# A hybrid trunk layer on one core: six more merge gates as seven-product pairs, their block differences formed on POOL and kept in DRAM

## The chip, the cores and the metric

The kernel runs on one core of a Trainium2 chip. The metric is the device time of one execution in microseconds (us), as the median of several runs. Engines are named as in the profile: PE (TensorE), DVE (VectorE), ACT (ScalarE), POOL (GpSimd) and SP, the queue that issues most DMAs.

## What is computed

One layer of width 1024 over 1024 positions. A combined projection feeds three causal mixers (stick-breaking attention "sb", gated DeltaNet "gdn", gated linear attention "gla") and three merge gates; the gated mixer outputs are projected, weighted by the merge gates, summed and projected again.

```python
h = rms_norm(x, norm_g) * (1 + scale) + shift
(sq, sk, sv, sz, dq, dk_, dv_, dz, db, da,
 lq, lk, lv, lz, lr, mg) = jnp.split(h @ w_in, offsets, axis=-1)   # mg: 3 * 1024 columns
y_sb, y_gdn, y_gla = ...          # the mixers, each times its silu gate; 512, 512, 1024 wide
g_sb, g_gdn, g_gla = jnp.split(jax.nn.sigmoid(mg + merge_b), 3, axis=-1)
merged = g_sb * (y_sb @ proj_sb) + g_gdn * (y_gdn @ proj_gdn) + g_gla * (y_gla @ proj_gla)
return x + gate * (merged @ w_out)
```

## The kernel before

Activations lie transposed: a tile has 128 channels as partitions and 1024 positions as columns, HS being its two halves of 512. Every fp32 operand of a large product is split into a rounded part `hi` (a cast on ACT, L151) and the rest `lo` (a subtraction on DVE, L152), and a product is three matmuls, hi·hi, hi·lo and lo·hi. `h_hi` and `h_lo` are the eight split tiles of h. Weights come as raw tiles of 256 KB (8 buffers) and are split into `w` tiles.

Work comes in *dense groups*: projection columns (`D.…`), merge gates (`gate(gi, d)`: 128 columns of one of the three gates, two halves of 24 matmuls, evacuated on ACT in L1182, sigmoid in L1187, kept in DRAM as `g_dram`), and the groups of the end. The mixers' small chained steps (`G.…` gdn, `L.…` gla, `S.m0` to `S.m3` sb) run at the same time. `emit` walks a clock of its own through the program and puts pieces of dense groups as filler between the mixers' steps; only PE's order is fixed by it, the other engines' by the order of the code and a scheduler. `dense` loads one group ahead. `FILL` says how many of the 24 gates are put at ten places of that stream; the ones that are left belong to `final_groups`, which run only when `S.m3` is done, so with no mixer beside them: the left gates, with `gla_operands` in between; four `gla_pair`; eight `proj_group` of proj_gdn, eight of proj_sb, and four `out_pair`.

A *pair* (`strassen`) computes two row blocks of 128 output channels at once with seven block products instead of eight: the four weight blocks are combined on DVE (`part`: s1 to s4), the right side is given as seven *units* (b11, t1, t2, b22, t3, b21, t4) a block p of four, a unit being hi and lo of 128x512. A pair has 7 × 12 = 84 matmuls. `combine` forms the units of one block with four subtractions and seven splits. In `gla_operands` it reads the four quarters from `y_dram`, where the mixers left their outputs. In `proj_group` of proj_sb with d of 4 and more it makes the units of `out_pair` from the merged tiles. `load_y` fetches and splits the four tiles that proj_gdn or proj_sb multiplies, in halves by way of two `mid` tiles. In `proj_group` each half is multiplied by its gate (L1366) and added to the merged tile (L1367), both on DVE.

Where the prediction follows steps of a mixer: in gla, L907 to L920 are DVE's elementwise work of the level steps, L1006 and L1008 the state's update in the scan, L292 is a power (reciprocal root) on POOL and L805 its multiplication on DVE; in sb, L1123/L1124 are activations on ACT, L1125 a scan over the keys on DVE, L1127 a product, L122 transposes on PE, L1148 their copies to SBUF on DVE, then the products with v (`mx`).

Of the kernel before, what the change touches and what calls it, by code (L numbers as in the profile page):

```python
# [52 lines left out]
def kernel(ctx: ExitStack, tc: tile.TileContext, xT: bass.AP, c: bass.AP,  # L53
# [1153 lines left out]
    def combine(b11, b12, b21, b22, unit, t1, t2):  # L1207

        out = {}

        def put(name, src):
            u = out[name] = unit(name)
            split(u[:, 0:HALF], u[:, HALF:2 * HALF], src)

        put("b11", b11)
        nc.vector.tensor_sub(out=t1, in0=b12, in1=b11)
        put("t1", t1)
        nc.vector.tensor_sub(out=t2, in0=b22, in1=t1)
        put("t2", t2)
        put("b22", b22)  # L1220
        nc.vector.tensor_sub(out=b12, in0=b22, in1=b12)
        put("t3", b12)
        put("b21", b21)
        nc.vector.tensor_sub(out=b21, in0=b21, in1=t2)
        put("t4", b21)
        return out

    def strassen(src, n1, n2, rhs, prepare, read):
# [75 lines left out]
    def gla_operands(p):  # L1304
        def run(_):
            raws = []
            for k in (p, p + 4):
                for sl, tag in zip(HS, ("v2", "v3")):
                    t = mid(tag)
                    nc.sync.dma_start(out=t, in_=y_dram[8 + k][:, sl])  # L1310
                    raws.append(t)
            gla_c[p] = combine(*raws, lambda name: unit_tile(GLA_TAGS[name][p]),
                               mid("v4"), mid("v4"))
            return
            yield
        return (lambda: None), run
# [4 lines left out]

# [198 lines left out]
```

## Time and profile before

| | |
|---|---|
| runs | 1523.69, 1524.74, 1530.83 us; median 1524.74 |
| profiled execution | 1526.96 us, span 1525.2 |
| busy PE / DVE / ACT / POOL | 1452.1 / 932.1 / 698.8 / 170.5 us |
| granted TensorE clock, mean | 0.982 of full speed |
| mixers alone with dense filler | to about 1184 us of the span |
| gates left, gla pairs, proj_gdn, proj_sb, out pairs | to 1249, 1339, 1392, 1443 and 1525 us |

Busy times are sums over the whole span; what one stage is limited by is read from its own stretch, by the waits that end last there.

### The profile page before, as it was taken

Reading aid. Unit: us, or ns where it says so; the run is one execution under the profiler, and the core shown is the slowest. Engines: PE = TensorE matmul, PEld = TensorE weight load, DVE = VectorE, ACT = ScalarE, POOL = GpSimd, SP = SyncE. Lnnn points to the kernel's source line nnn. Section 1 sums busy time; section 2 is a strip of 40 time slices with the busy share of each in tenths; the row PEclk is TensorE's granted clock in tenths of the full one; section 3 lists DMA queues with packets and bytes.
Section 4 is the critical chain, followed back from the end, with each engine's and each line's share of the span. In section 5 each row is a group of like instructions: output and inputs, shape, how many; then the busy total and the mean of one; then the engine's idle time right before and its main releaser. Section 6 shows DMA issues by size and latency. Waiting matters only on the chain.

```text
span 1525.2 us, 26640 instructions
## 1 busy us (share of the span) xinstructions
PE 1452.1 (95%) x10468; PEld 1211.1 (79%) x10468; DVE 932.1 (61%) x1930; ACT 698.8 (46%) x1483; POOL 170.5 (11%) x307
## 2 busy tenths in 40 slices
PE   4898999999999999999999999999999989989898
PEld 1687787777778887979788999999988867868687
DVE  6988737566643756666666525563655347577973
ACT  5165835453643746566476524342433344332321
POOL 4221222222330000000000100000000000000000
PEclk8899999999999999999999999999999998999999
DMA  6743322231322111111212221111123334474351
GB/s 223 218 125 112 99 80 74 57 81 47 90 83 60 39 47 56 46 55 38 73 43 60 66 56 36 49 50 45 40 63 101 114 115 117 132 230 125 111 162 66
DMA packets 169383, 132.77 MB, mean 87 GB/s; under 512 B 24197, under 2 KB 140037, under 8 KB 169258
## 3 DMA queue, kind: packets, MB, share of 16 engines
q1 hardware_dynamic: 169114, 130.76, 29.6%
q8 instruction: 82, 1.34, 0.4%
q14 instruction: 43, 0.35, 0.1%
q10 hardware_dynamic: 144, 0.31, 0.1%
HBM read 102.94 MB, written 28.10 MB: 86 GB/s over the span
## 4 chain that ended last, share of the span: by engine, by line
PE 76%; DVE 11%; DMA 5%; ACT 4%; POOL 2%; issue 2%; SPq 0%; DVEq 0%; POOLq 0%; ACTq 0%
PE acc L95 62%; PE lv L95 6%; PE mx L95 5%; PE tr L122 2%; DMA u<-in_adaT 1%; DVE u L307 1%; DVE w L152 1%; DVE w L583 1%; DVE u L394 1%; DVE w L581 1%; DMA v<-y_dram 1%; DMA v<-gam_d 1%; DMA w<-xd 1%; POOL c L292 1%; POOL u L464 1%
## 5 line engine op out<-in xcount | busy, mean ns | idle before, releaser
L95 PE MATMUL acc<-h_hi,w 128*128 128x512 f32 x1856 | 656.5, 408 | 11.0 <-ACT h_hi L364 7.0
L95 PEld LDWEIGHTS acc<-h_hi,w 128*128 128x128 f32 x1856 | 351.7, 189 | 82.9 <-issue 8.0
L95 PE MATMUL acc<-h_lo,w 128*128 128x512 f32 x928 | 365.8, 394 | 9.4 <-DVE h_lo L366 7.8
L151 ACT CAST w<-raw 128x512 fp32r<-128x512 f32 x231 | 140.9, 619 | 234.2 <-PE acc L95 203.4
L95 PE MATMUL acc<-w,h_hi 128*128 128x256 f32 x1280 | 238.8, 287 | 0.0
L152 DVE TENSOR_TENSOR w<-raw,w 128x512 fp32r<-128x512 f32 x231 | 159.7, 699 | 128.4 <-ACT w L151 123.2
L95 PEld LDWEIGHTS acc<-h_lo,w 128*128 128x128 f32 x928 | 176.6, 190 | 38.8 <-DVE h_lo L366 9.0
L95 PEld LDWEIGHTS acc<-w,h_hi 128*128 128x128 f32 x1280 | 198.7, 191 | 1.5 <-issue 0.7
L95 PE MATMUL acc<-u,w 128*128 128x512 f32 x696 | 179.0, 406 | 18.3 <-ACT u L151 12.7
L95 PE MATMUL acc<-w,h_lo 128*128 128x256 f32 x640 | 180.7, 282 | 0.0
L95 PEld LDWEIGHTS acc<-u,w 128*128 128x128 f32 x696 | 134.1, 194 | 54.3 <-ACT u L151 18.1
L95 PEld LDWEIGHTS acc<-w,h_lo 128*128 128x128 f32 x640 | 122.1, 191 | 0.0
L292 POOL TENSOR_TENSOR c<-c,mhalf 128x4 f32<-128x4 f32 (+1 forms) x56 | 54.9, 980 | 597.7 <-DVE c L290 573.3
L95 PE MATMUL acc<-unit,w 128*128 128x512 f32 x360 | 92.2, 394 | 0.0
L95 PEld LDWEIGHTS acc<-unit,w 128*128 128x128 f32 x360 | 67.9, 189 | 15.6 <-ACT v L1329 0.3
L1182 ACT ACTIVATE v<-acc,col 128x512 f32<-128x512 f32 x48 | 32.9, 685 | 81.1 <-PE acc L95 80.6
L1125 DVE TENSOR_TENSOR_SCAN u<-u,zero_c 128x128 f32<-128x128 f32 (+7 forms) x32 | 43.4, 1357 | 41.1 <-ACT u L1123 41.1
L95 PEld LDWEIGHTS mx<-r,u 128*128 128x128 f32 x288 | 44.1, 190 | 18.4 <-DVE r L762 4.9
L95 PE MATMUL mx<-r,u 128*128 128x128 f32 x288 | 48.5, 281 | 6.8 <-DVE r L762 2.4
L95 PE MATMUL lv<-u,u 128*32 128x32 f32 (+5 forms) x528 | 48.7, 250 | 2.2 <-DVE u L664 2.2
L95 PEld LDWEIGHTS lv<-u,u 128*32 128x32 f32 (+2 forms) x528 | 40.1, 145 | 11.1 <-issue 6.6
L286 ACT COPY u<-acc 128x512 f32<-128x512 f32 x50 | 29.0, 581 | 42.0 <-PE acc L95 41.4
(270 smaller groups left out, 2009.3 us busy)
## 6 DMA issues: line engine op xcount, KB each, us to landing
raw<-in_w_in SPq DMA_DIRECT2D x160, 256.0 KB, 3.1
u<-in_adaT SPq DMA_DIRECT2D x24, 512.0 KB, 4.0
g_dram<-v SPq DMA_DIRECT2D x48, 256.0 KB, 2.2
v<-g_dram SPq DMA_DIRECT2D x48, 256.0 KB, 2.9
v<-y_dram SPq DMA_DIRECT2D x32, 256.0 KB, 3.5
u<-in_xT SPq DMA_DIRECT2D x8, 512.0 KB, 8.0
v<-gam_d SPq DMA_DIRECT2D x16, 256.0 KB, 3.2
y_dram<-v SPq DMA_DIRECT2D x16, 256.0 KB, 2.0
```

What stands on the lines that cost most here:

```text
L95: return nc.tensor.matmul(out, lhsT=lhsT, rhs=rhs, **kw)
L122: nc.tensor.transpose(out=out, in_=in_, identity=ident[:k, :k])
L151: nc.scalar.copy(out=hi, in_=raw)
L152: nc.vector.tensor_sub(out=lo, in0=raw, in1=hi.bitcast(F32))
L286: nc.scalar.copy(out=dst[:, sl], in_=ps)
L292: nc.gpsimd.tensor_tensor(out=out, in0=out, in1=mhalf[:, 0:n], op=ALU.pow)
L307: nc.vector.tensor_tensor_reduce(out=junk, in0=aw, in1=c_row, scale=1.0, scalar=0.0, op0=ALU.mult, op1=ALU.add, accum_out=mod[:, j:j + 1])
L394: nc.vector.scalar_tensor_tensor(out=t, in0=r[:, tap:tap + T], scalar=C("conv", j + tap), in1=t, op0=ALU.mult, op1=ALU.add)
L464: nc.gpsimd.tensor_scalar(out=gt[0][DA, sl], in0=raw[DA, :], scalar1=C("dt_bias")[DA, :], scalar2=None, op0=ALU.add)
L581: nc.vector.tensor_tensor(out=t3, in0=L3[:, w:16, j:w].broadcast_to([32, n, w]), in1=Xl3[:, j:w, 0:w].broadcast_to([32, n, w]), op=ALU.mult)
L1125: nc.vector.tensor_tensor_scan(om[:, 0:n][:, ::-1], om[:, 0:n][:, ::-1], zero_c.broadcast_to([P, n]), 1.0, ALU.mult, ALU.add)
L1182: nc.scalar.activation(out=g, in_=ps, func=AF.Identity, bias=C("merge_b", gi * 8 + d))
```

## The change

Four of the eighteen gates that were filler leave the mixers: two behind the last gla columns (FILL[6]), one behind D.S0, one behind D.S2. Of the ten gates now left for `final_groups` four stay plain, two ahead of and two behind three `gate_pair`, each of which computes two gates with the seven products. Their units need differences of quarters of h: `T.h0` to `T.h3` form them on POOL during the mixers (four additions, since h is kept split, and four subtractions a block) and write them to DRAM; `T.y0` to `T.y3` do the same for the gla outputs (four loads, four subtractions). `h_operands` (put ahead of the first plain gate) and `gla_operands` (in two waves, 19 units ahead of the third plain gate and 9 ahead of gla pair 0) then load each unit's raw quarter straight into the place of its lo part and split it there. `load_y` does so with whole tiles. In proj_sb the merged add of d below 6 goes from DVE to POOL, and t4 of the out units is formed in t2's tile.

```diff
-FILL = (5, 1, 4, 0, 0, 0, 2, 1, 1, 4)
+FILL = (5, 1, 4, 0, 0, 0, 0, 0, 0, 4)
+PLAIN = (2, 2)
...
+    def load_unit(tag, src):
+        hi, lo = new_unit(tag)
+        raw = lo.bitcast(F32)
+        nc.sync.dma_start(out=raw, in_=src)
+        nc.scalar.copy(out=hi, in_=raw)
+        nc.vector.tensor_sub(out=lo, in0=raw, in1=hi.bitcast(F32))
+        return hi, lo
...
+    def differences(n, p, get):
+        def flat():
+            return raw_tile().rearrange("p k n -> p (k n)")
+        def sub(out, a, b, t):
+            nc.gpsimd.tensor_sub(out=out, in0=a, in1=b)
+            nc.sync.dma_start(out=t_dram[n, p][t], in_=out)
+        b12, b11 = get(flat(), 0, 1), get(flat(), 0, 0)
+        sub(b11, b12, b11, "t1")
+        b22 = get(flat(), 1, 1)
+        sub(b12, b22, b12, "t3")
+        sub(b22, b22, b11, "t2")
+        b21 = get(flat(), 1, 0)
+        sub(b21, b21, b22, "t4")
...
+    def h_differences(p):
+        def get(out, i, j):
+            k, sl = p + 4 * i, HS[j]
+            nc.gpsimd.tensor_add(out=out, in0=h_hi[k][:, sl].bitcast(F32),
+                                 in1=h_lo[k][:, sl].bitcast(F32))
+            return out
+    def y_differences(p):
+        def get(out, i, j):
+            nc.sync.dma_start(out=out, in_=y_dram[8 + p + 4 * i][:, HS[j]])
+            return out
...
+    def h_operands():
+        for p in range(4):
+            h_c[p] = {name: (h_hi[k][:, sl], h_lo[k][:, sl])
+                      for name, k, sl in (("b11", p, HS[0]), ("b21", p + 4, HS[0]),
+                                          ("b22", p + 4, HS[1]))}
+        for t in ("t1", "t2", "t3", "t4"):
+            for p in range(4):
+                h_c[p][t] = load_unit(H_TAGS[t][p], t_dram["h", p][t])
...
+    def gate_pair(e1, e2):
+        ...
+        return strassen(*cols_, h_c, dict, read)
...
         for k, tag in enumerate(Y_TAGS[yi]):
             a, b = unit_tile(tag), unit_tile(tag)
-            for sl, v in zip(HS, ("v2", "v3")):
-                yr = mid(v)
-                nc.sync.dma_start(out=yr, in_=y_dram[yi + k][:, sl])
-                split(a[:, sl], b[:, sl], yr)
+            raw = b.bitcast(F32)
+            nc.sync.dma_start(out=raw, in_=y_dram[yi + k])
+            nc.scalar.copy(out=a, in_=raw)
+            nc.vector.tensor_sub(out=b, in0=raw, in1=a.bitcast(F32))
...
                 nc.vector.tensor_mul(out=t, in0=g[hf], in1=ps)
-                nc.vector.tensor_add(out=merged[d][:, sl], in0=merged[d][:, sl], in1=t)
+                add = nc.gpsimd if gi == 0 and d < 6 else nc.vector
+                add.tensor_add(out=merged[d][:, sl], in0=merged[d][:, sl], in1=t)
...
-        late = [gate(*e) for e in EARLY[sum(FILL):]]
-        gs = [late[0], gla_operands(0), gla_operands(1), late[1], gla_operands(2),
-              gla_operands(3)] + late[2:] + [gla_pair(p) for p in range(4)]
+        late = EARLY[sum(FILL):]
+        plain = [gate(*e) for e in late[:PLAIN[0] + PLAIN[1]]]
+        pairs = late[sum(PLAIN):]
+        gs = [after(h_operands, plain[0])] + plain[1:PLAIN[0]]
+        gs += [gate_pair(*pairs[i:i + 2]) for i in range(0, len(pairs), 2)]
+        gs += [after(lambda: gla_operands(FIRST_UNITS), plain[PLAIN[0]])] + plain[PLAIN[0] + 1:]
+        gs += [after(lambda: gla_operands(("t3", "b21", "t4")), gla_pair(0))]
+        gs += [gla_pair(p) for p in range(1, 4)]
...
+    for p in range(4):
+        tasks.append((f"T.h{p}", lambda p=p: h_differences(p), [f"D.Lv{p}"], 0))
+        tasks.append((f"T.y{p}", lambda p=p: y_differences(p), ["L.s3.1", f"D.S{min(p, 2)}"], 0))
```

On PE, between the last gla columns and the first sb columns, the gla steps (`lv`, `mx`) stood in before with matmuls of a gate (`acc<-h…`) between them:

```order
L95 MATMUL lv<-v_9179 32x32 x16
L95 MATMUL acc<-h_hi,w 128x512
L95 MATMUL acc<-h_lo,w 128x512
L95 MATMUL acc<-h_hi,w 128x512 x2
L95 MATMUL acc<-h_lo,w 128x512
L95 MATMUL acc<-h_hi,w 128x512
L95 MATMUL mx<-w_9203,u_8915 128x256
L95 MATMUL mx<-w_9204,u_8915 128x256
```

and now stand one behind the other:

```order
L96 MATMUL acc<-w,h_hi 128x256 x2
L96 MATMUL acc<-w,h_lo 128x256
L96 MATMUL lv<-v_9186 64x64 x4
L96 MATMUL mx<-u_8860,u_9005 128x256
L96 MATMUL mx<-u_8861,u_9005 128x256
L96 MATMUL mx<-u_8860,u_9006 128x256
L96 MATMUL lv<-v_9221 32x32 x8
L96 MATMUL mx<-w_9251,u_9005 128x256
```

The two gates have gone from this place, and nothing has come instead. (Lines of the changed kernel are one higher here: L96 is L95 of before.)

On PE at the end of `S.m0`, the first sb mixer, the transposes (`tr`, and `mx<-cst`) and products with v of the last key blocks had gate matmuls between them before:

```order
L122 MATMUL tr<-cst,u_10722 128x128 x4
L122 MATMUL mx<-cst,u_10722 128x128 x4
L95 MATMUL acc<-h_hi,w 128x512
L95 MATMUL acc<-h_lo,w 128x512
L95 MATMUL acc<-h_hi,w 128x512 x2
L95 MATMUL mx<-v_10851,u_10021 128x128 x4
L95 MATMUL mx<-v_10858,u_10022 128x128 x4
```

and now follow each other until the next sb columns (`acc<-w,h_hi`):

```order
L123 MATMUL tr<-cst,u_10690 128x128 x4
L123 MATMUL mx<-cst,u_10690 128x128 x3
L96 MATMUL mx<-v_10792,u_9991 128x128 x4
L96 MATMUL mx<-v_10798,u_9992 128x128 x3
L123 MATMUL tr<-cst,u_10748 128x128 x4
L123 MATMUL mx<-cst,u_10748 128x128 x4
L96 MATMUL mx<-v_10812,u_9991 128x128 x4
L96 MATMUL mx<-v_10819,u_9992 128x128 x4
L96 MATMUL acc<-w,h_hi 128x256 x2
```

The matmuls of one gate have moved behind the mixers from here.

On DVE in proj_sb, at the first out block, the multiplications that empty PE's banks (`v<-v,acc`, L1366) alternated in before with the merged adds (L1367) and the block's operations:

```order
L1366 TENSOR_TENSOR v_14478<-v_14446,acc 128x512
L152 TENSOR_TENSOR w<-raw,w 128x512
L1367 TENSOR_TENSOR unit<-unit,v_14478 128x512
L1218 TENSOR_TENSOR v_14482<-unit,v_14481 128x512
L1221 TENSOR_TENSOR unit<-unit 128x512
L1366 TENSOR_TENSOR v_14530<-v_14513,acc 128x512
L152 TENSOR_TENSOR unit<-v_14482,unit 128x512
L152 TENSOR_TENSOR unit<-unit 128x512 x3
L1367 TENSOR_TENSOR unit<-unit,v_14530 128x512
```

and now (L1423 is that multiplication, L1444 to L1450 the block's subtractions):

```order
L1423 TENSOR_TENSOR v_14643<-v_14611,acc 128x512
L153 TENSOR_TENSOR w<-raw,w 128x512
L1446 TENSOR_TENSOR v_14647<-unit,v_14646 128x512
L1449 TENSOR_TENSOR unit<-unit 128x512
L153 TENSOR_TENSOR unit<-v_14647,unit 128x512
L153 TENSOR_TENSOR unit<-unit 128x512
L1450 TENSOR_TENSOR v_14647<-unit,v_14647 128x512
L153 TENSOR_TENSOR unit<-unit 128x512 x2
L153 TENSOR_TENSOR unit<-v_14647,unit 128x512
L1423 TENSOR_TENSOR v_14695<-v_14678,acc 128x512
```

The merged adds have left this queue, and the block's operations stand together between two of the multiplications.

## Rows read from the trace of the kernel before

**Rows 1.** Page, busy time by engine.
```profile
PE 1452.1 (95%) x10468; PEld 1211.1 (79%) x10468; DVE 932.1 (61%) x1930; ACT 698.8 (46%) x1483; POOL 170.5 (11%) x307
```

**Rows 2.** Stretches: us, busy PE, PEld, DVE, ACT, POOL, clock, DMA share, GB/s.
```profile
1249.21:1338.80 89.59, 80.88 (x335) 64.36 (x334) 61.21 (x97) 36.12 (x63) 0.00 (x0) 0.92 0.47 139
1339.25:1392.00 52.75, 48.01 (x194) 37.30 (x193) 35.56 (x56) 13.00 (x22) 0.00 (x0) 0.94 0.62 188
1392.00:1443.46 51.46, 46.58 (x193) 36.92 (x192) 47.09 (x77) 18.06 (x31) 0.00 (x0) 0.97 0.38 115
```

**Rows 3.** Waits of PE from 880 us on: total us, times, longest.
```profile
PE acc L95 <- ACT u L151: 12.7, 4, 6.0
```

**Rows 4.** Timeline of PE in gla pair 0: start, us, instructions, wait before.
```profile
1249.21 1.56 PE L95 MATMUL acc<-u,w 128*128 128x512 f32 x6
...
1261.50 11.73 PE L95 MATMUL acc<-u,w 128*128 128x512 f32 x39 [5.99 <-ACT u L151]
```

**Rows 5.** Timeline of PE in proj_gdn (first row) and proj_sb.
```profile
1342.76 0.50 PE L95 MATMUL acc<-u,w 128*128 128x512 f32 x1 [2.64 <-ACT u L151]
...
1422.77 3.55 PE L95 MATMUL acc<-u,w 128*128 128x512 f32 x9 [2.70 <-DVE v L1366]
```

**Rows 6.** Timeline of ACT: gate evacuations, gla pairs' first copies, proj_gdn casts.
```profile
1227.65 0.69 ACT L1182 ACTIVATE v<-acc,col 128x512 f32<-128x512 f32 x1 [2.10 <-PE acc L95]
...
1233.09 0.69 ACT L1182 ACTIVATE v<-acc,col 128x512 f32<-128x512 f32 x1 [3.71 <-PE acc L95]
...
1284.38 0.59 ACT L1329 COPY v<-acc 128x512 f32<-128x512 f32 x1 [2.14 <-PE acc L95]
...
1303.66 0.59 ACT L1329 COPY v<-acc 128x512 f32<-128x512 f32 x1 [2.10 <-PE acc L95]
...
1364.50 0.62 ACT L151 CAST w<-raw 128x512 fp32r<-128x512 f32 x1 [3.41 <-PE acc L95]
1370.04 0.62 ACT L151 CAST w<-raw 128x512 fp32r<-128x512 f32 x1 [4.91 <-PE acc L95]
```

**Rows 7.** Stretches, columns as in rows 2.
```profile
812.70:844.24 31.54, 31.54 (x327) 25.05 (x326) 20.37 (x47) 21.86 (x39) 1.96 (x5) 1.00 0.30 85
...
1255.00:1260.00 5.00, 0.51 (x2) 0.00 (x0) 4.92 (x9) 3.24 (x6) 0.00 (x0) 0.50 0.84 254
...
500.00:600.00 100.00, 99.40 (x987) 83.00 (x987) 66.01 (x156) 61.70 (x116) 5.24 (x12) 1.00 0.18 49
```

**Rows 8.** Timeline of DVE: three operations back to back.
```profile
1407.72 1.89 DVE L152 TENSOR_TENSOR unit<-unit 128x512 fp32r<-128x512 f32 x3
```

**Rows 9.** Timeline at 168.8 us: a POOL operation and DVE's beside it.
```profile
168.81 0.16 DVE L581 TENSOR_TENSOR w<-w,w 32x15 f32<-32x15 f32 x1
...
168.91 1.29 POOL L731 TENSOR_TENSOR u<-u,v 128x512 f32<-128x512 f32 x1 [1.72 <-ACT v L730]
...
169.00 1.23 DVE L583 TENSOR_TENSOR w<-w,w 32x15 f32<-32x15 f32 x1
```

**Rows 10.** Groups of DVE, 812.70 to 844.24: busy, mean ns, idle before and releaser.
```profile
L152 DVE TENSOR_TENSOR w<-raw,w 128x512 fp32r<-128x512 f32 x6 | 4.1, 686 | 0.7 <-ACT w L151 0.7
L152 DVE TENSOR_TENSOR w<-r,w 128x256 fp32r<-128x256 f32 x4 | 1.9, 481 | 3.2 <-ACT w L151 3.2
...
L805 DVE TENSOR_SCALAR v<-v,c 128x256 f32<-128x256 f32 x4 | 1.2, 352 | 1.5 <-POOL c L292 1.5
```

**Rows 11.** Timeline at the end of S.m3: scores, scan, product, copies, products with v.
```profile
1158.22 1.55 PE L95 MATMUL lv<-u,u 128*128 128x512 f32 x6
...
1160.73 2.29 DVE L1125 TENSOR_TENSOR_SCAN u<-u,zero_c 128x1024 f32<-128x1024 f32 x1 [2.31 <-ACT u L1123]
1163.12 1.23 DVE L1127 TENSOR_TENSOR u<-u,u 128x1023 f32<-128x1023 f32 x1
...
1170.95 0.69 DVE L1148 COPY v<-tr 128x512 f32<-128x512 f32 x1 [3.42 <-PE tr L122]
...
1173.95 1.95 PE L95 MATMUL mx<-v,u 128*128 128x128 f32 x16
```

More of the change, by code (lines that the diff above doesn't have):

```diff
@@ L1205, with strassen @@
     UNITS = ("b11", "t1", "t2", "b22", "t3", "b21", "t4")
[L1207 to L1228, printed above, removed]
+    def strassen(src1, src2, rhs, prepare, read, before=None):
         def load():
             a = {}
-            for key, k0, n in (("11", 0, n1), ("21", 0, n2), ("22", 4, n2), ("12", 4, n1)):
-                a[key] = load_raw(src[:, n * P:(n + 1) * P], k0)
+            for key, k0, src in (("11", 0, src1), ("21", 0, src2), ("22", 4, src2), ("12", 4, src1)):
+                a[key] = load_raw(src, k0)
             ws = []
@@ L1263, in run @@
             for i, unit in enumerate(UNITS):
+                if before is not None:
+                    before(i)
                 if i + 3 < 7:
@@ L1302, in unit_tile, with new_unit @@
                        bufs=3 if tag == "u5" else 2)[:, 0:T]
[L1304 to L1316, printed above, removed]
+    def new_unit(tag):
+        u = unit_tile(tag)
+        return u[:, 0:HALF], u[:, HALF:]
@@ new lines, in load_unit @@
+    def load_unit(tag, src):
[5 more added lines that the diff above has]
+        return hi, lo
+    t_dram = {(n, p): {t: dp.tile([P, HALF], F32, name=f"{n}{t}_{p}") for t in ("t1", "t2", "t3", "t4")}
+              for n in "hy" for p in range(4)}
+    def differences(n, p, get):
[11 more added lines that the diff above has]
+        sub(b21, b21, b22, "t4")
+        return
+        yield
@@ new lines, in gate_pair, with read @@
+    def gate_pair(e1, e2):
+        cols_ = [w_in[:, O_MG + gi * D + d * P:O_MG + gi * D + (d + 1) * P] for gi, d in (e1, e2)]
+        def read(i, ps, c):
+            if i < 3:
+                r = c[i] = mid(("v2", "v3", "v1")[i])
+                nc.scalar.copy(out=r, in_=ps)
+                return
+            b = {3: (0, 1), 4: (1, 1), 5: (0, 0), 6: (1, 0)}[i]
+            if i < 6:
+                g = r = c[{3: 2, 4: 1, 5: 0}[i]]
+                nc.vector.tensor_add(out=r, in0=r, in1=ps)
+            else:
+                r, g = ps, mid("v0")
+            gi, d = (e1, e2)[b[0]]
+            nc.scalar.activation(out=g, in_=r, func=AF.Sigmoid, bias=C("merge_b", gi * 8 + d))
+            nc.sync.dma_start(out=g_dram[gi, d][:, HS[b[1]]], in_=g)
+        return strassen(*cols_, h_c, dict, read)
@@ new lines, in gla_operands @@
+    def gla_operands(names):
+        for name in names:
+            for p in range(4):
+                if name[0] == "t":
+                    src = t_dram["y", p][name]
+                else:
+                    src = y_dram[8 + p + 4 * (name[1] == "2")][:, HS[name[2] == "2"]]
+                c = gla_c.setdefault(p, {})
+                if name not in c and (GLA_TAGS[name][p] != "h") == (names is FIRST_UNITS):
+                    c[name] = load_unit(GLA_TAGS[name][p], src)
+    FIRST_UNITS = ("b11", "t1", "t2", "b22", "t3")
@@ L1337, in read @@
             nc.vector.tensor_mul(out=block(p, *b), in0=c["g"][b[0]][b[1]], in1=r)
-        return strassen(proj_gla, p, p + 4, gla_c, prepare, read)
+        return strassen(*(proj_gla[:, d * P:(d + 1) * P] for d in (p, p + 4)), gla_c, dict, read)
     ys = {}
```

64 lines of the change are left out of this document (45 added, 19 removed).

## Prediction

> **What bounds the kernel now.** I read the page first, then the table of stretches of the last 300 us, the waits of TensorE there, and the timelines at its long waits; last the mixers' rows at the two places where filler leaves. TensorE (PE) is busy 1452.1 of 1525.2 us [rows 1], so a change can win in two ways only: fewer matmuls, or fewer waits of PE. Nearly all waits lie behind the mixers. The reader should see three of them, stretch by stretch [rows 2]. The four gla pairs last from 1249.21 to 1339.25, 90.0 us. An undisturbed pair takes 1303.66 − 1284.38 = 19.28 us [rows 6], four take 77.1: loss 12.9. Its largest wait is 5.99 us, for the ACT half of an operand's split, which releases PE four times for 12.7 us in all [rows 3, 4]. The proj_gdn groups take 52.75 us; one takes 1370.04 − 1364.50 = 5.54 [rows 6], eight 44.3: loss 8.5, again with ACT's split as releaser [rows 5]. The proj_sb groups take 51.46, loss 7.1, and there the releaser is DVE's multiply in front of the merged add [rows 5]: VectorE is busy 47.09 of 51.46 us [rows 2]. Together 28.5 us, part of it at half clock: the granted clock was 0.50 in 1255 to 1260 (1.2 GHz) after PE had waited, and 1.00 (2.4 GHz) in stretches without waits [rows 7].
>
> **The change part by part.** The sum is made against the profiled execution, 1526.96 us; the median of the runs, 1524.74, is 2.2 lower.
>
> *Gate pairs.* A gate half of 24 matmuls takes 1233.09 − 1227.65 = 5.44 us [rows 6], a gate 10.88. Six took 65.3; three pairs of the gla pair's 84 matmuls take 57.8. Gain **7.4**, all of it on PE's path, since these groups run behind the mixers where nothing else feeds PE.
>
> *gla operands.* The combine (four subtractions and seven splits a block, four blocks) leaves the place; 19 + 9 units are loaded, each a 256 KB transfer, one cast on ACT and one subtraction on DVE. DVE does three operations back to back in 1.89 us [rows 8], 0.63 each, so 19 units are 12 us of DVE beside plain gate 3, plain gate 4 and more (21.8 us of PE): hidden, unless the loads start late. They stand on SP behind the weight loads of proj_gla, and the split of gla weights stands behind the casts of the units. I take 2.2 for the first wave and 1.3 for the second, 3.5 in all, between 0 and the 12.9 of now. Gain **9.4**.
>
> *load_y.* 512 KB transfers, one cast and one subtraction for each instead of two, and no intermediate tiles that must come free. Left 2, between 0 and 8.5. Gain **6.5**.
>
> *proj_sb.* Twelve merged adds go from DVE to POOL, minus 12 × 0.63 = 7.6 us of DVE. But a POOL tensor operation of 128x512 stops DVE: POOL's ran 1.29 us from 168.91, and beside it DVE's 32x15 operation took 1.23 [rows 9]; the operation of that form just ahead took 0.16, so DVE lost about 1.05. Twelve such cost up to 12.6. The out operands must also wait for the POOL add; in the new order DVE then does nine operations of one pair's operands between two evacuations. The Trainium skill ("SBUF — State Buffer", section "SBUF: two separate sides") speaks against this edit: the port pair that DVE and GpSimd share is an exclusive lock, held for the whole instruction, and the loser stands still; the two rows agree with it. By bounds: −7.1 (loss gone) to +8 (12.6 − 7.6 plus 3 of waiting). I take **3.8 lost**, nearer the upper end, because DVE is the releaser there.
>
> *The first thinned stretch (812.70 to 844.24).* Two gates leave: 96 × 5.44/24 = 21.8 us of PE. PE was busy all 31.54 us, so 9.8 us of mixer work is left, and the order shows no dense matmul between the GLA steps. What is late next is the GLA chain on DVE. DVE was busy 20.37 us there [rows 7], less four gate splits of 0.69 [rows 10]: 17.6. Low: DVE never waits, 17.6 − 9.8 = 7.8. High: it keeps all its idle time, 31.54 − 20.37 = 11.2, so 28.8 − 9.8 = 19. Its waits for ACT and POOL in this stretch are 3.2 and 1.5 [rows 10]; these hardly shrink when PE's queue empties, those for PE do. I keep 4.1 of them: 21.7 − 9.8 = 11.9, and 1.1 for matmuls at a lower clock. **Cost 13**, 8 to 19.
>
> *The end of S.m0.* The gate there leaves, and its last scores, transposes and products stand without filler. The last block of S.m3 gives durations [rows 11]: scores from 1158.22, scan ends and multiply starts 1163.12 (4.9), multiply 1.23, transposes about 1.2, two copies 1.3, sixteen products 1.95, together 10.6; the preceding block's transposes, copies and products stand ahead in between, an estimate of 2.7 from the same rows: 13.3 us from scores to the last product. PE works 1.55 (scores), about 2.2 (transposes) and 42 × 0.122 = 5.1 (products of three blocks), 8.9: 4.4 idle. One POOL operation of T.y1 in it adds 1, and half clock over some 5 us, as in 1255 to 1260, 2.4. **Cost 8** (4.4 + 1 + 2.4 = 7.8), 4 to 11. The gate that leaves behind D.S2 has its place taken by projection columns in the order: nothing.
>
> *The end of S.m3.* The 16 units of h are cast and subtracted while the last block runs; six subtractions stand on DVE ahead of its copies, 6 × 0.63 = 3.8 us, less what PE has queued. **Cost 2.5**, 1 to 5.
>
> *The 48 POOL operations.* 48 × 1.29 = 62 us of POOL, which is idle enough, but each can hold DVE for 1.05. DVE is busy 66% in 500 to 600 [rows 7], so about 48 × 0.66 × 1.05 = 33 us of delay, spread over eight bursts. Level steps have some us of slack before PE misses them, scan steps have none. 0 if all of it falls into DVE's idle third; 14 if each of the four T.h bursts holds one scan step for 3.5. SP's queue and the `raw` tiles come in too: a write waits on SP for its POOL operation with weight loads behind it, and a burst holds four of the eight `raw` tiles; the loads are a group ahead (10.88 us), which covers a burst of five (6.5 us). The rsqrt powers on POOL stand behind up to three operations, 3.9 us, with DVE's L805 waiting for them [rows 10]. **Cost 4.**
>
> *Sum.* Gains 7.4 + 9.4 + 6.5 = 23.3. Costs 3.8 + 13 + 8 + 2.5 + 4 = 31.3. Net +8.0: 1526.96 + 8.0 = 1535.0, on the median's basis 1532.7. I forecast **1533**.
>
> **The rivals.**
> *A, faster:* the thinned stretch closes at DVE's bare work (8), S.m0 at its low end (4), S.m3 at 1, the bursts fall in idle time (0), proj_sb stays as it is, and the operand waits vanish. One mechanism decides it: whether DVE alone, not DVE and ACT in turn, sets the GLA steps once PE's queue is empty; below a stretch of about 17 us gates there were pure surplus. Gains 7.4 + 12.9 + 8.5 = 28.8, costs 13: −16, **1509**. For it: PE is busy to the last tenth there, so surplus can't be read directly. Against: DVE does wait for ACT there, 3.2 us over four operations [rows 10].
> *B, POOL's lock rules:* the bursts cost 14 and proj_sb 8: 1533 + 10 + 4 = **1547**. For it: the stopped DVE operation in rows 9. Against: a third of DVE's time is free.
> By the same page of the Trainium skill the lock concerns every DVE operation with two SBUF operands; by that rule alone B would be nearer, but no row shows how often PE misses the delay.
> *C, the change doesn't do what it says:* the loads of units queue behind weight loads on SP and behind casts on ACT, and the waits of pair 0 and of load_y are merely elsewhere. Of the 15.9 gained there 7 are left: **1542**. For it: ACT was the releaser, and ACT still casts every unit. Against: 19 of 28 units have two gates' time.
>
> **How the numbers follow.** Forecast 0.42, spread 1525 to 1541. A 0.27, B 0.16, C 0.15. A measurement of this kernel tells about 0.5%, 7.6 us, from no change: 1517 to 1532.4. The forecast case lies half on either side of 1532.4 (0.20 same, 0.22 slower); A gives 0.23 faster and 0.04 same; B all slower; C 0.12 slower, 0.03 same. Faster 0.23, same 0.27, slower 0.50. The range reaches down to A's better half and up through C and most of B: **1506 to 1549**.
>
> **What would show it.** Gate pairs: ACT copies of the gate pairs 19.3 us apart. The thinned stretch: PE waits of 10 to 13 us in all between the last D.Lv matmul and the first of D.S0, released by DVE, at a clock below 1. S.m0: waits for DVE's transposed copies. POOL's lock: DVE operations of 1.5 us and more beside the bursts. gla pair 0 without a wait above 2 us. The forecast is wrong if the first thinned stretch lasts under 18 us or over 29 us, or if proj_sb takes less than 50 us.

## The result, and the profile after

The change makes the kernel slower: 1541.91 us as the median of five runs (1539.24 to 1543.44), against 1528.11 of the kernel before in the same session; ratio 1.0092, 95% interval 1.0069 to 1.0115. The forecast was 1533 in a range of 1506 to 1549, 8 us above the kernel before; the measured rise is 13.8. The profiled execution after has a span of 1540.3 us, 15.1 more than before.

The page's busy line answers [rows 1]: PE works no longer than before, DVE 31 and POOL 92 us more.

```profile
PE 1450.5 (94%) x10432; PEld 1209.4 (79%) x10432; DVE 963.1 (63%) x1940; ACT 704.7 (46%) x1493; POOL 262.4 (17%) x367
```

The stretches of the end answer [rows 2] (us; busy PE, PEld, DVE, ACT, POOL; granted clock; DMA share; GB/s): the three gate pairs, the gla pairs, proj_gdn and proj_sb.

```profile
1194.97:1252.90 57.93, 57.75 (x252) 46.73 (x251) 29.44 (x45) 31.01 (x53) 0.00 (x0) 1.00 0.52 158
1275.03:1353.86 78.83, 78.12 (x337) 62.76 (x336) 51.38 (x76) 33.97 (x56) 0.00 (x0) 1.00 0.57 181
1353.86:1398.60 44.74, 44.44 (x194) 35.99 (x193) 31.70 (x47) 6.97 (x10) 0.00 (x0) 1.00 0.54 171
1398.60:1457.43 58.83, 49.04 (x192) 38.16 (x191) 44.42 (x66) 17.93 (x31) 20.55 (x12) 0.92 0.31 101
```

The gla pairs fell from 90.0 to 78.8 us and proj_gdn from 52.75 to 44.74, both all but free of waits. proj_sb rose from 51.46 to 58.83, with POOL busy 20.55 us on twelve adds, 1.71 each in the mean.

The stretch where two gates left answers the first of [rows 7]: from the last gla columns' matmul to the first of D.S0, and the 4 us behind it.

```profile
819.60:842.63 23.03, 13.69 (x230) 11.01 (x230) 17.94 (x43) 9.75 (x25) 2.26 (x5) 0.72 0.21 58
842.63:846.62 3.99, 3.99 (x20) 3.99 (x19) 1.57 (x3) 1.21 (x4) 0.00 (x0) 0.50 0.22 72
```

PE stands idle for 9.3 of the 23.0 us.

The waits of PE from 500 us on answer [rows 3]; ACT's casts of units are gone from it, and in their place stand DVE's steps of the mixers and proj_sb's multiply, L1423 now (us in total, times, longest).

```profile
PE acc L96 <- DVE v L1423: 10.1, 5, 4.0
PE mx L96 <- DVE v L1149: 5.5, 4, 2.0
PE tr L123 <- DVE u L153: 3.3, 1, 3.3
PE tr L123 <- DVE v L952: 3.0, 2, 2.2
PE mx L96 <- ACT w L152: 2.7, 3, 1.8
```

To place the mixers' loss I set the same DVE instruction of both traces side by side. Before (the last L789 of gdn, a GLA step, the first product of S.m0 and the first of S.m1):

```profile
508.72 0.74 DVE L789 SCALAR_TENSOR_TENSOR v<-tr,col,u 128x512 f32<-128x512 f32 x1
...
797.86 0.68 DVE L951 TENSOR_TENSOR v<-v,u 128x512 f32<-128x512 f32 x1
...
911.86 0.29 DVE L1127 TENSOR_TENSOR u<-u,u 128x127 f32<-128x127 f32 x1
...
978.78 0.29 DVE L1127 TENSOR_TENSOR u<-u,u 128x127 f32<-128x127 f32 x1
```

and after:

```profile
509.84 0.74 DVE L790 SCALAR_TENSOR_TENSOR v<-tr,col,u 128x512 f32<-128x512 f32 x1
...
803.62 0.69 DVE L952 TENSOR_TENSOR v<-v,u 128x512 f32<-128x512 f32 x1 [1.25 <-ACT v L951]
...
912.04 0.29 DVE L1128 TENSOR_TENSOR u<-u,u 128x127 f32<-128x127 f32 x1
...
973.81 0.29 DVE L1128 TENSOR_TENSOR u<-u,u 128x127 f32<-128x127 f32 x1
```

A distance after, minus the distance before, plus the matmuls of the gates that left (10.88 us a gate), is what a part lost:

| part | forecast | measured | from |
|---|---|---|---|
| up to the last L789 | 0 | +1.1 | 509.84 − 508.72; nothing is changed there |
| GLA beside T.h0 to T.h2 | in the +4 of all bursts | +4.6 | 293.8 against 289.1 |
| last GLA steps to S.m0 | +13 | +16.2 | 108.4 against 114.0, plus 21.8 |
| S.m0 | +8 | +5.7 | 61.8 against 66.9, plus 10.9 |
| S.m1 to the first late gate | +2.5 | +4.8 | 199.1 (to 1172.9) against 205.2 (to 1249.21 − 65.3 = 1183.9, six gates ahead of the gla pairs), plus 10.9 |
| gate pairs | −7.4 | −7.4 | 57.93 against six gates, 65.3 |
| gla pairs | −9.4 | −11.2 | 78.83 against 90.04 |
| proj_gdn | −6.5 | −8.0 | 44.74 against 52.75 |
| proj_sb | +3.8 | +7.4 | 58.83 against 51.46 |
| out pairs to the end | 0 | +1.1 | 82.9 against 81.7 |

The sum is +14.3. The four plain gates, 44.2 us against 43.5, bring it to 15.0 of the 15.1 by which the spans differ.

### The profile page after: what moved, and what is told of

Read it like the earlier page. It is cut to its first block, busy times and chain, and to the rows that moved or that the text cites. A ratio compares the mean times of both kernels' runs of the same rounds, so it can differ in the third digit from the quotient of the medians.

```text
span 1540.3 us, 26825 instructions
## 1 busy us (share of the span) xinstructions
PE 1450.5 (94%) x10432; PEld 1209.4 (79%) x10432; DVE 963.1 (63%) x1940; ACT 704.7 (46%) x1493; POOL 262.4 (17%) x367
## 4 chain that ended last, share of the span: by engine, by line
PE 63%; DVE 16%; DMA 6%; ACT 6%; POOL 5%; issue 5%; SPq 0%; DVEq 0%; POOLq 0%; ACTq 0%
PE acc L96 50%; PE mx L96 5%; PE lv L96 5%; PE tr L123 2%; DVE w L153 2%; DVE w L584 1%; DVE u L308 1%; DVE w L582 1%; DVE u L395 1%; POOL c L293 1%; POOL unit L1425 1%; DMA u<-in_adaT 1%; POOL raw L1292 1%; DMA v<-gam_d 1%; DMA w<-xd 1%
## 5 line engine op out<-in xcount | busy, mean ns | idle before, releaser
L96 PE MATMUL acc<-h_hi,w 128*128 128x512 f32 x1736 | 615.9, 408 | 12.5 <-ACT h_hi L365 7.0
L96 PEld LDWEIGHTS acc<-h_hi,w 128*128 128x128 f32 x1736 | 328.5, 189 | 79.9 <-issue 8.0
L96 PE MATMUL acc<-h_lo,w 128*128 128x512 f32 x868 | 341.6, 394 | 9.1 <-DVE h_lo L367 7.8
L153 DVE TENSOR_TENSOR w<-raw,w 128x512 fp32r<-128x512 f32 x240 | 168.8, 712 | 119.0 <-ACT w L152 112.0
L96 PE MATMUL acc<-w,h_hi 128*128 128x256 f32 x1280 | 240.4, 288 | 0.9 <-DVE u L153 0.9
L96 PE MATMUL acc<-u,w 128*128 128x512 f32 x888 | 218.4, 398 | 11.0 <-DVE v L1423 10.1
L96 PEld LDWEIGHTS acc<-u,w 128*128 128x128 f32 x888 | 167.9, 190 | 52.8 <-DVE v L1423 5.2
L96 PEld LDWEIGHTS acc<-w,h_hi 128*128 128x128 f32 x1280 | 200.2, 193 | 2.5 <-DVE u L153 1.1
L96 PEld LDWEIGHTS acc<-h_lo,w 128*128 128x128 f32 x868 | 164.9, 190 | 36.7 <-DVE h_lo L367 9.0
L96 PE MATMUL acc<-w,h_lo 128*128 128x256 f32 x640 | 181.5, 284 | 0.0
L293 POOL TENSOR_TENSOR c<-c,mhalf 128x4 f32<-128x4 f32 (+1 forms) x56 | 55.3, 987 | 408.9 <-DVE c L291 392.4
L96 PEld LDWEIGHTS acc<-w,h_lo 128*128 128x128 f32 x640 | 123.0, 192 | 0.0
L96 PE MATMUL acc<-unit,w 128*128 128x512 f32 x312 | 81.0, 397 | 0.5 <-DVE v L1471 0.5
L1425 POOL TENSOR_TENSOR unit<-unit,v 128x512 f32<-128x512 f32 x12 | 20.6, 1722 | 350.4 <-DVE v L1423 350.4
L96 PEld LDWEIGHTS acc<-unit,w 128*128 128x128 f32 x312 | 59.3, 191 | 14.7 <-DVE v L1471 0.9
L96 PEld LDWEIGHTS mx<-r,u 128*128 128x128 f32 x288 | 44.2, 190 | 19.1 <-DVE r L763 5.3
L1292 POOL TENSOR_TENSOR raw<-raw 128x512 f32<-128x512 f32 x32 | 46.1, 1440 | 62.6 <-DMA raw<-y_dram 61.1
L96 PE MATMUL mx<-r,u 128*128 128x128 f32 x288 | 48.4, 280 | 7.5 <-DVE r L763 2.8
L96 PE MATMUL lv<-u,u 128*32 128x32 f32 (+5 forms) x528 | 48.7, 250 | 4.3 <-DVE u L665 4.2
```

What stands on the lines that cost most here:

```text
L96: return nc.tensor.matmul(out, lhsT=lhsT, rhs=rhs, **kw)
L153: nc.vector.tensor_sub(out=lo, in0=raw, in1=hi.bitcast(F32))
L293: nc.gpsimd.tensor_tensor(out=out, in0=out, in1=mhalf[:, 0:n], op=ALU.pow)
L1292: nc.gpsimd.tensor_sub(out=out, in0=a, in1=b)
L1425: add.tensor_add(out=merged[d][:, sl], in0=merged[d][:, sl], in1=t)
```

## The experiments

Theory after the result: two separate losses, of about the same size as the gains. Gates that had been filler were the only work that PE had in two chains (the empty places), and work on POOL takes more of DVE's time than it saves (POOL's lock). The rival for each is the other one: that the thinned stretch is slow because T.h3 holds DVE there, or that proj_sb is slow by its order alone. A third reading has no run of its own, but the traces speak to it: that work on POOL costs because other things stand in order behind it, and not because DVE is stopped (POOL's queue). All but one kernel compute the whole layer; that one is named. Ratios are to the kernel before in the same session.

**e1, the two gates behind the last gla columns go back.**

```diff
-FILL = (5, 1, 4, 0, 0, 0, 0, 0, 0, 4)
+FILL = (5, 1, 4, 0, 0, 0, 2, 0, 0, 4)
```

> Two gates go back behind the last gla columns (FILL[6] = 2); eight gates are left behind the mixers, four plain and two pairs. Theory of the empty place: the stretch from the last gla columns to the first sb scores cost 16 us only because nothing stood between the GLA steps; it comes back, less 2.5 us for one gate pair that turns plain: about 1528 us, PE waits of under 3 us in that stretch. Theory of POOL's lock: the stretch is slow because T.h3 and T.y0 hold DVE there; gates between the steps give back little, 1538 to 1544 us.

1526.57 us, ratio 0.9983 (0.9969 to 0.9996): 15 us come back, though one pair fewer takes 2.5 of the gain. The stretch has no wait worth naming:

```profile
820.00:850.00 30.00, 30.00 (x322) 24.05 (x323) 18.63 (x43) 21.54 (x39) 2.02 (x5) 1.00 0.30 83
```

PE is busy all 30 us at full clock, and between the two DVE instructions of the table the last GLA steps take 113.99 us, as before the change (114.00). The empty place is the cause there. POOL is no rival for it: in either kernel it is busy for only about 2 us of this stretch, since T.h3 has run ahead of it (in the changed kernel it ends at 800 us).

**e2, the merged adds of proj_sb go back to DVE.**

```diff
-                add = nc.gpsimd if gi == 0 and d < 6 else nc.vector
+                add = nc.vector
```

> The merged adds of proj_sb all run on DVE again; nothing else is changed. If POOL's adds are what made proj_sb 7.4 us longer (58.8 against 51.5), it falls back to about 51 to 53 us and the run to about 1535. If the gathered order of the out operands alone did it, proj_sb stays above 57 us and DVE's twelve additional adds make it longer: 1542 to 1548.

1535.17 us, ratio 1.0041 (1.0028 to 1.0054): 6.7 us less than the changed kernel. proj_sb itself falls further than expected, and part of it comes again as a wait at the first out pair. The stretch of proj_sb, and PE at the first out pair:

```profile
1396.97:1443.85 46.88, 45.22 (x194) 35.81 (x193) 44.46 (x72) 16.35 (x28) 0.00 (x0) 1.00 0.39 122
```
```profile
1453.94 1.63 PE L96 MATMUL acc<-unit,w 128*128 128x512 f32 x3 [4.44 <-DVE v L1471]
```

DVE does 72 operations in 46.9 us there; in the changed kernel it does 66 in 58.8 us and is busy for the same 44.4. So POOL's adds save DVE no time, but the stretch is longer because DVE waits. In the changed kernel, from 1398.60 to 1457.43, it waits for POOL's adds and for casts on ACT, some of which stand behind them (us in total, times, longest):

```profile
DVE u L153 <- ACT u L152: 5.9, 3, 2.9
DVE unit L153 <- ACT unit L152: 2.8, 2, 2.1
DVE v L1446 <- POOL unit L1425: 2.4, 2, 1.2
DVE v L1444 <- POOL unit L1425: 1.2, 1, 1.2
```

In e2 only 0.7 us of these 12.3 are left. Either engine also holds up the other. DVE's splits beside a POOL add take 1.40 or 1.41 and not 0.69, and POOL's add at 1445.60 lasts 4.06 us: DVE runs without a gap to 1448.53, and the add ends 1.13 us later. First DVE, then POOL, then ACT, then PE, all of the changed kernel:

```profile
1410.58 1.40 DVE L153 TENSOR_TENSOR w<-raw,w 128x512 fp32r<-128x512 f32 x1
...
1447.26 1.27 DVE L153 TENSOR_TENSOR u<-unit,u 128x512 fp32r<-128x512 f32 x2
1451.39 0.69 DVE L153 TENSOR_TENSOR u<-v,u 128x512 fp32r<-128x512 f32 x1 [2.85 <-ACT u L152]
```
```profile
1445.60 4.06 POOL L1425 TENSOR_TENSOR unit<-unit,v 128x512 f32<-128x512 f32 x1 [8.45 <-DVE v L1423]
```
```profile
1449.70 0.62 ACT L152 CAST unit<-unit 128x512 fp32r<-128x512 f32 x1 [3.16 <-POOL unit L1425]
```
```profile
1452.73 4.21 PE L96 MATMUL acc<-u,w 128*128 128x512 f32 x9 [4.04 <-DVE v L1423]
```

The chain is short: the add ends at 1449.66, ACT casts the sum and only then the operand that DVE's queue is waiting for at its head, and the multiply that empties PE's bank stands behind that.

**e3, the 48 operations on differences are left out.** The DMAs stay and carry undiffered blocks, so the gates of the pairs and the gla products are computed from other numbers; its time is that of the rest.

```diff
-            nc.gpsimd.tensor_sub(out=out, in0=a, in1=b)
-            nc.sync.dma_start(out=t_dram[n, p][t], in_=out)
+            nc.sync.dma_start(out=t_dram[n, p][t], in_=a)
...
-            nc.gpsimd.tensor_add(out=out, in0=h_hi[k][:, sl].bitcast(F32),
-                                 in1=h_lo[k][:, sl].bitcast(F32))
-            return out
+            return h_hi[k][:, sl].bitcast(F32)
```

> The 48 additions and subtractions of the block differences are left out (the DMAs stay and carry undiffered blocks, so the gates and gla products are computed from other numbers). If POOL's lock costs what the anchors say, 4.7 us between 509 and 798 us and a part of the two thinned places, the run takes 1533 to 1537. If the delays come from the empty places and the DMAs, 1540 to 1542.

1532.16 us, ratio 1.0017 (1.0003 to 1.0031): 9.7 us less than the changed kernel, a little more than expected. Between the same two instructions the GLA part takes 288 us, as before the change (289), and the thinned stretch to S.m0 is unchanged at 108. So the bursts on POOL cost the GLA steps 5 to 6 us, and the empty place has nothing to do with them. Not all of the 9.7 us is the differences' own: proj_sb is 4.0 us shorter in e3's trace than in the changed kernel's, though nothing was edited there. And with the operations the waits of SP and of the `raw` tiles for them are gone too; e10 and e11 keep those.

**e4, e1 and e2 together, and the gate behind D.S0 back (17 gates as filler).**

```diff
-FILL = (5, 1, 4, 0, 0, 0, 0, 0, 0, 4)
-PLAIN = (2, 2)
+FILL = (5, 1, 4, 0, 0, 0, 2, 1, 0, 4)
+PLAIN = (2, 1)
...
-                add = nc.gpsimd if gi == 0 and d < 6 else nc.vector
+                add = nc.vector
```

> Both edits, and the gate behind D.S0 goes back too (seven gates left: three plain, two pairs). By the empty place theory: 1541.9 - 16.2 (gla) - 5.7 (end of S.m0) - 6 (adds) + 2.5 (one pair fewer), about 1516 to 1520, under the kernel before. By the lock theory with the T operations kept: no better than 1534.

1522.22 us, ratio 0.9963 (0.9945 to 0.9981), below the kernel before, but 2 to 6 us above the expectation. e1 and e2 alone add up to 15.3 + 6.7 = 22.0, and the gate behind D.S0 was to bring 5.7 more; measured are 19.7 for the three. That gate brought nothing: from S.m0 to S.m1 e4 takes 72.8 us, 5.8 more than the kernel before (66.9) although the gate stands there again. So the loss in S.m0 is not that of the empty place alone; e8 shows what it is. The bursts still take 6 us in GLA.

**e5, all eighteen gates back as filler; one plain gate, two pairs, one plain gate; adds on DVE.**

```diff
-FILL = (5, 1, 4, 0, 0, 0, 0, 0, 0, 4)
-PLAIN = (2, 2)
+FILL = (5, 1, 4, 0, 0, 0, 2, 1, 1, 4)
+PLAIN = (1, 1)
...
-                add = nc.gpsimd if gi == 0 and d < 6 else nc.vector
+                add = nc.vector
```

> All eighteen filler gates stand where they stood before (FILL as before), six are left: one plain, two pairs, one plain; merged adds on DVE. If the empty places were the mixers' whole loss apart from the bursts on POOL: against the kernel before -5 (two pairs), -11 (gla operands), -8 (load_y), +2 (proj_sb and out pairs), +5 to +9 (POOL bursts): 1512 to 1518. If one plain gate is too little cover for the loads of units: waits of 3 to 6 us at the first gate pair or at gla pair 0, 1518 to 1524.

1520.10 us, ratio 0.9936 (0.9913 to 0.9959). Two to eight us above the expectation, though no wait at a gate pair or a gla pair is above 0.8 us: one plain gate is cover enough for the loads. What is left lies in the mixers, 6.2 us in GLA and 4.6 in S.m0, and in the wait of 4.4 at the first out pair that e2 has too.

**e6, as e4 with eight of the adds on POOL (d below 4), none straight ahead of an out block.**

```diff
-                add = nc.gpsimd if gi == 0 and d < 6 else nc.vector
+                add = nc.gpsimd if gi == 0 and d < 4 else nc.vector
```

> As e4, but the merged adds of d below 4 (four groups, eight adds, none straight ahead of an out block) run on POOL. If POOL's lock sets the price, proj_sb and the first out pair take 1 to 4 us longer than in e4 (132.9 us from the first proj_sb matmul of the fourth tile to the end): 1523 to 1526. If only the adds that the out operands wait for did harm, DVE is relieved, the wait of 4.4 us at the first out pair shrinks: 1518 to 1520.

1524.53 us, ratio 0.9963 (0.9943 to 0.9984). In time it can't be told from e4, whose ratio is the same; in the profile proj_sb with what follows takes 135.1 us against 132.9, and POOL has an add of 4.05 us again, with a wait of 3.52 behind it. A relief it is not; whether it does harm the times leave open.

**e7, as e5 with the differences of h beside the sb mixers.**

```diff
-        tasks.append((f"T.h{p}", lambda p=p: h_differences(p), [f"D.Lv{p}"], 0))
+        tasks.append((f"T.h{p}", lambda p=p: h_differences(p), [f"D.S{p}", f"T.y{p}"], 0))
```

> As e5, but the differences of h are formed beside the sb mixers (behind D.S and T.y of the same number) and not beside the GLA mixers. If the bursts cost the GLA steps what the anchors say, the 5 us between 509 and 798 us come back; the sb mixers with their long DVE scans take 0 to 5 of it: 1510 to 1517, 0 to 5 below e5. If the place doesn't matter: e5's time.

1525.07 us, ratio 0.9988 (0.9971 to 1.0005), 5 us above e5: the expectation missed to the wrong side. The GLA part does come back (289 us between the two instructions, 295 in e5), but the sb mixers pay more than that: from S.m0 to S.m3 they take 227.9 us against 219.2. PE's waits from 880 to 1200 us in e7:

```profile
PE tr L123 <- DVE v L1149: 5.4, 1, 5.4
PE tr L123 <- DVE u L1128: 4.9, 1, 4.9
```

**e8, as e5 without gate pairs: six plain gates, no T.h, none of its loads.**

```diff
-PLAIN = (1, 1)
+PLAIN = (3, 3)
...
-        gs = [after(h_operands, plain[0])] + plain[1:PLAIN[0]]
+        gs = plain[:PLAIN[0]]
...
-        tasks.append((f"T.h{p}", lambda p=p: h_differences(p), [f"D.Lv{p}"], 0))
```

> As e5, but without gate pairs: six plain gates, no differences of h, none of their loads; the two waves of gla units, load_y and T.y stay. Against e5: +5 for the two pairs, -5 for the four T.h bursts: 1513 to 1519, the same as e5 within 2 us. If the pairs are worth more than their differences cost, e8 is 3 to 6 us above e5; if less, 3 to 6 below.

1517.99 us, ratio 0.9926 (0.9902 to 0.9950): the same as e5 within the intervals. Two pairs are worth no more than their differences cost on POOL. e8 also shows the remaining loss best, late in S.m0. POOL, DVE and PE there, all of e8:

```profile
961.42 6.21 POOL L1292 TENSOR_TENSOR raw<-raw 128x512 f32<-128x512 f32 x3 [5.75 <-DMA raw<-y_dram]
...
962.86 1.89 DVE L1128 TENSOR_TENSOR u<-u,u 128x1023 f32<-128x1023 f32 x1
...
964.67 1.25 DVE L291 TENSOR_SCALAR c<-c 128x4 f32<-128x4 f32 x1
...
967.60 1.00 POOL L293 TENSOR_TENSOR c<-c,mhalf 128x4 f32<-128x4 f32 x1
...
968.64 0.69 DVE L1077 TENSOR_TENSOR v<-acc,c 128x512 f32<-128x512 f32 x1 [2.13 <-POOL c L293]
...
970.59 0.94 PE L123 MATMUL tr<-cst,v 128*128 128x128 f32 x4 [3.64 <-DVE v L1149]
```

The same place before:

```profile
960.70 0.16 DVE L290 TENSOR_SCALAR c<-c 128x4 f32<-128x4 f32 x1
...
961.00 1.31 POOL L292 TENSOR_TENSOR c<-c,mhalf 128x4 f32<-128x4 f32 x1 [8.62 <-DVE c L290]
...
962.35 0.69 DVE L1076 TENSOR_TENSOR v<-acc,c 128x512 f32<-128x512 f32 x1 [0.90 <-POOL c L292]
```

Three subtractions hold POOL for 6.2 us, 2.07 each beside DVE's operations and not 1.29; DVE's small operations stretch as well; the power of the sb columns waits behind the three; the multiply L1077 waits for the power; and every copy behind it on DVE waits with it, though none of them needs POOL.

**e9, as e8 with the sixteen gla subtractions on DVE; e10, as e5 with all 48 operations on DVE.**

```diff
-            nc.gpsimd.tensor_sub(out=out, in0=a, in1=b)
+            nc.vector.tensor_sub(out=out, in0=a, in1=b)
...
-            nc.gpsimd.tensor_add(out=out, in0=h_hi[k][:, sl].bitcast(F32),
+            nc.vector.tensor_add(out=out, in0=h_hi[k][:, sl].bitcast(F32),
```

(the second piece in e10 alone)

> As e8, but the sixteen subtractions of the gla differences run on DVE and not on POOL. In e8 three of them took 6.2 us on POOL at 961 us, the power of the sb columns stood behind them until 967.6, and with it DVE's next multiply and all copies behind that: PE waited 3.6 us and then ran slower. If POOL's queue and its lock are the cost, that wait goes, and sixteen DVE operations of 0.63 us cost less: 1512 to 1516. If any sixteen more operations beside the sb mixers cost the same: 1517 to 1521, e8's time, or more since DVE is busier than POOL.

> As e5, but all 48 operations on the differences of h and of the gla outputs run on DVE. By the lock theory each POOL operation took up to 1.05 us of DVE's time, on DVE itself it takes 0.63: 4 to 8 us below e5, 1512 to 1516. If DVE's own load in the GLA steps (67% busy) is the limit, no gain or a loss: 1519 to 1525.

e9: 1513.25 us, ratio 0.9909 (0.9888 to 0.9930). e10: 1509.58 us, ratio 0.9899 (0.9869 to 0.9930), the best kernel of this study, 1.0% below the kernel before. Both came out inside or below what the lock theory gave. e9 can't be told from e8 (0.9926) by the intervals, and those of e5 and e10 just overlap; against e5, e10 gains 5.6 us by the ratios and 10.5 by the medians. The clear case is e11 below. DVE is busier, and PE waits less; the stretches of e10 in GLA, and PE's waits from 500 to 910 us:

```profile
500.00:600.00 100.00, 99.62 (x1005) 83.17 (x1004) 73.15 (x168) 62.44 (x115) 5.13 (x12) 1.00 0.23 66
600.00:700.00 100.00, 99.62 (x1062) 83.72 (x1061) 71.40 (x161) 60.08 (x109) 4.84 (x11) 1.00 0.27 74
```
```profile
PE mx L96 <- DVE w L153: 1.1, 3, 0.4
PE tr L123 <- DVE w L1032: 1.0, 1, 1.0
```

e5 has these two waits and two larger ones ahead of them:

```profile
PE tr L96 <- PE lv L96: 2.9, 3, 1.0
PE lv L96 <- DVE v L915: 2.0, 3, 0.7
```

PE is busy 99.62 of 100 us in e10, with 73 us of DVE where 66 were before [rows 7]: DVE's idle third does take the operations, if they come through its own queue.

What the gain comes from, the traces show better than the times. Between the same two instructions, first the kernel before, then e5, then e10:

```profile
508.72:797.86 289.14, 288.00 (x3018) 242.77 (x3018) 190.89 (x439) 175.52 (x314) 13.02 (x31) 1.00 0.20 52
507.19:802.58 295.39, 288.68 (x3018) 242.86 (x3018) 196.39 (x438) 174.21 (x314) 54.26 (x60) 1.00 0.23 66
506.49:795.63 289.14, 287.99 (x3018) 242.80 (x3018) 208.42 (x468) 174.88 (x314) 12.95 (x31) 1.00 0.24 68
```

On POOL the operations of T.h raise DVE's busy time by 5.5 us, on DVE itself by 17.5. Yet e5 loses 6.2 us there and e10 nothing. So it is not, or not mainly, stopped DVE time that costs, as the lock theory has it, but what stands behind the operations in POOL's queue: the power L293, which DVE's multiply L806 needs. POOL and DVE in e5, then DVE in e10:

```profile
597.95 1.55 POOL L1308 TENSOR_TENSOR raw<-h_hi,h_lo 128x512 f32<-128x512 f32 x1
599.45 2.66 POOL L1292 TENSOR_TENSOR raw<-raw 128x512 f32<-128x512 f32 x2
602.08 0.71 POOL L293 TENSOR_TENSOR c<-c,mhalf 128x2 f32<-128x2 f32 x1
...
602.82 0.62 DVE L806 TENSOR_SCALAR v<-v,c 128x256 f32<-128x256 f32 x2 [4.47 <-POOL c L293]
```
```profile
597.90 0.62 DVE L806 TENSOR_SCALAR v<-v,c 128x256 f32<-128x256 f32 x2 [0.59 <-POOL c L293]
```

The power's operand is ready at 598.02, and three operations run ahead of it. The wait of 4.46 or 4.47 us comes three times in this stretch of e5, DVE's level steps up to L915 and PE's wait for that stand behind it, and in e10 it is 0.59 as before the change. It is a chain of the same kind as in e8.

**e11, the changed kernel with its own gate places, but all of POOL's new work on DVE.**

```diff
-            nc.gpsimd.tensor_sub(out=out, in0=a, in1=b)
+            nc.vector.tensor_sub(out=out, in0=a, in1=b)
...
-            nc.gpsimd.tensor_add(out=out, in0=h_hi[k][:, sl].bitcast(F32),
+            nc.vector.tensor_add(out=out, in0=h_hi[k][:, sl].bitcast(F32),
...
-                add = nc.gpsimd if gi == 0 and d < 6 else nc.vector
+                add = nc.vector
```

> The changed kernel with its own gate places (14 as filler), but all work that it gave to POOL (48 operations on differences, twelve merged adds) on DVE. Two costs add if they are separate: against the changed kernel's 1541.9 us, -6.7 for the adds (e2) and -9 to -10 for the differences (e3 left them out, e10 moved them for -10.5): 1524 to 1528, and what then remains against e10 is the empty places, 15 to 18 us. If DVE, which paces the emptied GLA stretch, gets longer by T.h3's operations there, 1528 to 1533.

1527.50 us, ratio 1.0000 (0.9989 to 1.0011), inside the expected 1524 to 1528. e11 differs from e2 in the 48 operations on differences alone: 1.0000 against 1.0041, with intervals well apart, 6.3 us by the ratios and 7.7 by the medians. So in the changed kernel the 60 operations on POOL cost 14 us over the same operations on DVE, and the empty places what remains against e10: 15 us by the ratios, 18 by the medians, and 2.5 more for the third pair that e11 has and e10 has not.

The parts of the mixers, each against the kernel before, by the distances of the table above (10.88 us a gate that left):

| kernel | filler gates | differences | GLA | last GLA steps | S.m0 |
|---|---|---|---|---|---|
| changed | gone | on POOL | +4.6 | +16.2 | +5.7 |
| e3 | gone | left out | −1.5 | +16.2 | +2.4 |
| e11 | gone | on DVE | −0.3 | +14.8 | +5.1 |
| e4 | back, but for the one behind D.S2 | on POOL | +6.2 | 0.0 | +5.8 |
| e5 | back | on POOL | +6.2 | 0.0 | +4.6 |
| e10 | back | on DVE | 0.0 | 0.0 | +0.6 |

The last GLA steps follow the gates and the GLA part follows POOL. In S.m0 either alone costs: the empty place 2.4 us, POOL's queue 4.6 to 5.8 with the gate in place. Where the place is empty, the operations cost there on DVE nearly what they cost on POOL.

## Why the forecast came out as it did

The sign was right, the size was 8 against 13.8, and of the mechanisms two were not what the forecast had: that of the 48 operations and, in part, that of S.m0. The signs named beforehand came nearly all: gate pairs 19.3 us apart, no wait above 0.4 us at gla pair 0, the thinned stretch and proj_sb inside their bounds, and a DVE operation of 1.89 us beside POOL (e8; 1.21 before). PE's waits in the thinned stretch were 9.3 us, just under the 10 to 13 given, 6.6 of them for DVE and 2.7 for ACT.

*The thinned stretch* was the best step: 21.7 us by DVE's bare work plus the waits for ACT and POOL, measured 23.0, with DVE busy 17.94 where 17.6 was forecast. Rival A, that the gates there were surplus, falls: DVE and ACT take turns, as its "against" said. The clock cost was undersized: 1.1, against 1.8 behind the stretch alone, where matmuls that took 2.24 us before took 3.99 at 0.50. With these the stretch costs 15.0; the remaining difference to 16.2 lies on either side of it.

*The gains.* The gate pairs gave the 7.4 to a tenth. The loads of units were hidden better than forecast: 1.7 us left of 12.9 (forecast 3.5), 0.4 of 8.5 (forecast 2). Rival C falls; ACT still casts every unit, but with two gates' time for it. One reading of before was wrong without harm to the sum: of the four waits for ACT's split, 12.7 us, two (8.5 us) lie in the gla pairs and two (4.2 us) in proj_gdn.

*proj_sb* was mis-sized, 3.8 for 7.4, near the upper bound of 8, and the bound was made of the wrong parts. I had up to 12.6 us of stopped DVE, less 7.6 saved, and 3 of waiting. DVE's busy time fell by 2.7 us, 47.09 to 44.42, so about 4.9 of the 7.6 were lost again and not 12.6; the waits for the adds and for the casts behind them were the larger part. The row at 168.91 [rows 9] shows a DVE operation that arrives second, and not a POOL operation that finds DVE busy without a gap: POOL's adds took 1.71 in the mean and one 4.06.

*The 48 operations* were put at 4 for all. Measured are 9.7 us against leaving them out (e3, up to 4.0 of it in proj_sb) and 6.3 to 7.7 against the same operations on DVE (e11 against e2): 4.6 in the GLA part of the changed kernel, and about 3 of the loss in S.m0 (5.7 against 2.4 in e3). The step that failed is the price by the lock: 33 us of delay for DVE, nearly all of it in DVE's idle third, and holes only at the scan steps. In e5 POOL's operations raised DVE's busy time in the GLA part by 5.5 us, and the loss came instead through the power on POOL: L806 waited 4.47 us behind three operations and not 0.59, and the level steps behind it, which the forecast gave some slack, reached PE late. The prediction names that path, with 3.9 us for three operations, but takes no price from it; in the sb mixers, where one multiply at the head of DVE's queue holds all copies behind it (e8), it does not name it. Rival B, at 14 for the bursts and 8 for proj_sb, was right about the size of proj_sb and too high for the bursts, and its reason, stopped DVE time, is not what the rows show. The rule of the Trainium skill ("SBUF — State Buffer", section "SBUF: two separate sides"), that the port pair shared by DVE and GpSimd is an exclusive lock, agrees with single rows, a split of 1.40 us beside POOL's add at 1410.13 and not 0.69. e9, e10 and e11 don't test it, since they empty POOL's queue as well.

*S.m0 and S.m3.* In S.m0 5.7 for 8 is near by luck. The empty place with its clock was put at 6.8 and POOL at 1; without POOL's operations the place costs 2.4 (e3), and with the gate back and POOL's operations kept nothing is gained (e4). That the gate behind D.S2 would leave no hole held for its own place. The 4.8 us from S.m1 on are 1.1 and 1.3 in S.m1 and S.m2, which had no term, and 2.5 in S.m3 as forecast, with two waits for copies (1.42 and 1.97) at its end.

Not settled: part of the difference between the profiled and the other executions lies in the first 500 us, which no edit touches (the last L789 lies between 506 and 515 us in the thirteen traces), so terms of 1 or 2 us are not to be trusted singly. No run parts POOL's lock from POOL's queue, say by moving only the powers off POOL; what is said of them rests on the rows of e5, e8 and e10. Why POOL's last add takes 1.68 us in e3 and 4.06 in the changed kernel is open too.
